# First feed-forward of a macaron layer in seven half products per gate/up tile, with its modulation vectors computed later

## Chip, cores and metric

One core of one Trainium2 chip runs the whole layer as one program. The metric is the time of one execution in microseconds (us), taken as the median of several; a profiled execution gives the rows shown below. TensorE (PE) multiplies, VectorE (DVE) and ScalarE (ACT) do the elementwise work, GpSimd (POOL) does some of it and issues a few DMAs, and SyncE (SP) issues most DMAs, in the order of its own queue.

## What is computed

The input is one sequence of 512 tokens with 1024 features in float32. Cut to what matters here:

```python
sc = silu(c)
mod = sc @ ada_w + ada_b                      # nine vectors of 1024: sh1 sc1 g1 sh2 sc2 g2 sh3 sc3 g3
y = rmsnorm(h, ffn1_pre_g) * (1 + sc1) + sh1
y = (silu(y @ w_gate) * (y @ w_up)) @ w_down  # 1024 -> 2816 -> 1024
h = h + 0.5 * g1 * rmsnorm(y, ffn1_post_g)
...                                           # token mixing with sh2 sc2 g2
...                                           # a second feed-forward with sh3 sc3 g3
```

The two feed-forwards have the same shapes and other weights. Matrix products keep nearly float32 accuracy by splitting each operand in a rounded part and a rest (hi, lo) and adding three products: hi·hi, hi·lo, lo·hi.

## The kernel before

**Three multiplications for one.** `mm3` (L112) issues three matmuls, at L113, L114 and L115. `unit` (L97) loads 512 KB of weights on SP's queue into one of four `raw` buffers (pool `wraw`), casts them to `hi` on ACT (L108) and subtracts to `lo` on DVE (L109); `hi` and `lo` have four buffers each in the pool `wsp`.

**Order of work.** The kernel is written as one program; a scheduler places the instructions of each engine from that order and from when it thinks that data are ready, so instructions of a later step can stand ahead of those of an earlier one. On each engine they run strictly in the order placed. The `GAP_` constants pad pools and so shift addresses.

**Modulation vectors.** `ada(s, kind, j)` (L120) makes 128 entries of one vector: one DMA of 512 KB into a `raw` buffer, four multiply-and-sum instructions on DVE (L134) and one reduction (L138). There are 72 of them. `ada_scale` (L140), `gate_rows` (L146, writes the gate vector to DRAM) and `gate_load` (L154, reads it back for all partitions into the buffer `G`) finish a vector.

**First feed-forward** (`ffn1`, L313).
- Start: `prep(k)` (L324) makes feature block k of y from two `ada` calls, transposes on PE and two ACT instructions (L332, L334); the lo part follows on DVE (L335). Meanwhile the six gate/up blocks of the first three of 22 tiles of 128 hidden features (`START_F = 3`) are multiplied block by block (`first`, L339; results `ps_s`). Their weights park in `wsp` buffers and their split parts in the tail of `hT`.
- 19 further tiles (`up_tile`, L235): two weight blocks of 1024x128, 48 matmuls with 512 columns each (`pua`). `swiglu_evac` (L224) applies sigmoid and two multiplications and splits the result at once into `hT[0]` and `hT[1]`. After each tile one entry of the list `rest` runs, at some two: 24 entries in all, most of them an `ada`.
- `down` (L244): the output columns in two halves, each of 11 units of two hidden tiles by four token blocks (24 matmuls of 512 columns a unit). Each unit takes another entry of `rest`.

**Token mixing** (`mix`, L399): 24 projections `pft` of 24 matmuls each, between which chains of small steps for eight heads run on all engines (`level`, L612, with DVE L602 and L591 and POOL L603). Eight `ada` calls lie among them.

**Second feed-forward** (`ffn2`, L812): three tiles are made directly, with 256 columns at a time (`pub`). The other 19 use seven products of halves (`Tile`, L886): each of the seven is 4 blocks of 128 by `mm3` on 256 tokens, so 84 matmuls of 256 columns a tile. Needed for that are sums of quarters of y (`sums`, L833, into `Shi`, `Slo`; `sum4`, L858), sums of quarters of the weights (`prep1` to `prep5`, L913 to L936), and sums of the results (L946 to L974). The loop (L994) prepares tile v while it multiplies tile w:

```python
w.p6(); ...load...; v.prep1(); w.p5(); v.prep2(); w.p7(); v.prep3()
v.open(); v.p1(); v.p2(); v.prep4(); w.p4(); v.prep5(); w.p3()
```

The last two products (`p4`, `p3`) of the last tile are issued within `down`. There `hT` is one float32 tile, and `split` (L1025) makes hi and lo of two hidden tiles for each of the 22 units; the same two tiles are split again for the second half.

Of the kernel before, what the change touches and what calls it, by code (L numbers as in the profile page):

```python
# [7 lines left out]
F32 = mybir.dt.float32  # L8
F32R = mybir.dt.float32r
# [18 lines left out]
GAP_H = 128  # L28
# [6 lines left out]
def layer_kernel(ctx: ExitStack, tc: tile.TileContext, x, c, cols, gate_b,  # L35
# [48 lines left out]
    nc.scalar.activation(sg, crow, AF.Sigmoid)  # L84
    nc.vector.tensor_tensor(out=crow, in0=crow, in1=sg, op=ALU.mult)
    for q in range(2):
        pc = tr_tile(f"pc{q}")
        nc.tensor.matmul(pc, ident[0:2, q:q + 1].broadcast_to([2, P]), crow, start=True, stop=True)
        nc.vector.tensor_copy(sc[:, q * T:(q + 1) * T], pc)
# [134 lines left out]
    def swiglu_evac(f, psg, psu, hT, tag):  # L224
        t = small.tile([P, T], F32, tag="x2", name=f"t{tag}_{f}")
        nc.scalar.activation(t, psg, AF.Sigmoid)
        nc.vector.tensor_tensor(out=t, in0=t, in1=psg, op=ALU.mult)  # L227
        nc.vector.tensor_tensor(out=t, in0=t, in1=psu, op=ALU.mult)
        nc.scalar.copy(hT[0][:, f, :], t)
        nc.vector.tensor_tensor(out=hT[1][:, f, :], in0=t, in1=hT[0][:, f, :].bitcast(F32), op=ALU.subtract)  # L230

# [3 lines left out]
    def up_tile(f, wgu, y, hT, tag):  # L235
        us = [k3(unit(wgu[f, g], 1024, f"{tag}_{f}_{g}")) for g in range(2)]
        ps = [mm_tile(f"pu{tag}_{f}_{g}") for g in range(2)]
        for g in range(2):
            for k in range(KT):
                mm3(ps[g], (us[g][0][:, k, :], us[g][1][:, k, :]), (y[0][:, k, :], y[1][:, k, :]),  # L240
                    k == 0, k == KT - 1)
        swiglu_evac(f, ps[0], ps[1], hT, tag)

    def down(wd, hT, tag, s, nxt, n=NF, order=lambda f: f, pump=None, drain=None, rest=(), split=None):  # L244


        t0, ss0, later = [], [], []
        nu = n // 2
        for half in range(2):
# [12 lines left out]
            for u in range(nu):  # L262
                v = unit(wd[half, u], 1024, f"d{tag}_{half}_{u}")
# [3 lines left out]
                for _ in range(2 if split and u < 3 else 1):  # L267
                    if rest:
                        rest.pop(0)()
# [26 lines left out]
        return later  # L296
# [16 lines left out]
    def ffn1():  # L313
        with tc.tile_pool(name="hT1", bufs=1) as hp:
            phase(hp, "gap_h1", GAP_H)
            hT = (hp.tile([P, NF, T], F32R, name="hThi1"), hp.tile([P, NF, T], F32R, name="hTlo1"))
# [3 lines left out]
            for v in range(2 * START_F):  # L320
                sl = slice(NF - 2 * (v + 1), NF - 2 * v)
                dst.append(tuple(a[:, sl, :].rearrange("p a b -> p (a b)") for a in hT))

            def prep(k):  # L324
# [20 lines left out]
            def load(v, half):  # L345
                sl = slice(half * 512, (half + 1) * 512)
                unit(wgu1[v // 2, v % 2, :, sl], 512, f"s{v}_{half}", tuple(d[:, sl] for d in dst[v]),
                     park=("hi", "lo")[v % 2])

            nv = 2 * START_F  # L350
# [29 lines left out]
            for f in range(START_F):  # L380
                swiglu_evac(f, ps[2 * f], ps[2 * f + 1], hT, "a")
            rest = [lambda j=j: ada(0, 2, j) for j in range(KT)] + [lambda: gate_rows(0), lambda: ada(1, 0, 0), lambda: gate_load(0)]
            for s in (1, 2):
                rest += [lambda s=s, j=j, kind=kind: ada(s, kind, j) for kind in range(2) for j in range(KT)
                         if s + kind + j > 1]
                rest.append(lambda s=s: ada_scale(s))
# [5 lines left out]
            y2 = y_tiles(1)  # L392
            later = down(wd1, hT, "a", 0, (1, y2), rest=rest)
            while rest:
                rest.pop(0)()
        return y2, later


    def mix(y, later):  # L399
        with ExitStack() as mc:  # L400
# [388 lines left out]
            rest = [lambda j=j: ada(1, 2, j) for j in range(KT)] + [lambda: gate_rows(1), lambda: None, lambda: gate_load(1)]  # L789
            h_qf(0)  # L790
            for hd in range(NH):
                m_qk(hd)
                rest.pop(0)()
                h_g(hd)
                m_g(hd)
                rest.pop(0)()
                if hd + 1 < NH:
                    h_qf(hd + 1)
# [8 lines left out]
            y3 = y_tiles(2)  # L807
            later = down(w_out, (mhi, mlo), "m", 1, (2, y3), n=KT, order=order, pump=pump, drain=drain, rest=rest)
# [307 lines left out]
```

## Time and profile before

| what | value |
|---|---|
| median of three runs | 1036.87 us (1036.12 to 1037.81) |
| profiled execution, its own time | 1035.53 us |
| its span, first to last instruction | 1033.8 us |
| PE busy | 1011.2 us, 98% |
| DVE busy | 699.1 us, 68% |
| ACT busy | 431.0 us, 42% |
| granted TensorE clock, mean | 0.996 of full speed |

A busy share is an average over stages. A stage is bounded by the engine that has no idle time there; another engine's work costs nothing as long as it ends before the first one asks for it. An instruction's shown duration overlaps the next one's by some 0.07 to 0.1 us on DVE and ACT, and by much more on PE, so the distance between starts is what an instruction costs in a row of its kind.

### The profile page before, as it was taken

The numbers are of one execution on the slowest core, as the hardware profiler recorded it, in microseconds if no ns is written. First come the engines' busy times: TensorE is split into PE (matmuls) and PEld (weight loads), VectorE is DVE, ScalarE is ACT, GpSimd is POOL, SyncE is SP. The second block draws the span as 40 slices with busy tenths as digits, with TensorE's granted clock in tenths as the row PEclk, the third lists the DMA queues.
The fourth block names the chain that finished last, engine by engine and source line by source line (L and its number), as shares of the span: only waits on it lengthen the run. The fifth ranks groups of instructions, "written<-read, shape, count | busy, mean of one in ns | idle before, by whom it ended". The sixth has DMA issues, their size and how long they took to land.

```text
span 1033.8 us, 14910 instructions
## 1 busy us (share of the span) xinstructions
PE 1011.2 (98%) x5672; PEld 873.7 (85%) x5672; DVE 699.1 (68%) x1577; ACT 431.0 (42%) x694; POOL 86.6 (8%) x123
## 2 busy tenths in 40 slices
PE   6999999999999999999999999999999999999997
PEld 4788888888888887978888887889999999988886
DVE  7986455556655466279787786599687877983643
ACT  5532322332212155344434232466566666552531
POOL 1000000000000011012222222010010110000000
PEclk9999999999999999999999999999999999999999
DMA  9865444545554503253222421243445545563312
GB/s 344 281 220 159 143 163 135 171 151 173 188 200 147 170 34 116 90 174 133 80 85 101 104 82 42 62 144 94 114 130 143 133 125 140 159 200 122 102 42 81
DMA packets 45683, 141.49 MB, mean 137 GB/s; under 512 B 7974, under 2 KB 8358, under 8 KB 45612
## 3 DMA queue, kind: packets, MB, share of 16 engines
q1 hardware_dynamic: 42588, 135.41, 39.5%
q0 software_dynamic: 2736, 4.98, 3.1%
q8 instruction: 44, 0.72, 0.3%
q14 instruction: 27, 0.22, 0.1%
q10 hardware_dynamic: 288, 0.16, 0.1%
HBM read 138.41 MB, written 2.12 MB: 136 GB/s over the span
## 4 chain that ended last, share of the span: by engine, by line
PE 84%; DVE 9%; DMA 2%; issue 2%; ACT 1%; POOL 1%; DVEq 0%; POOLq 0%; SPq 0%; ACTq 0%
PE pua L114 7%; PE pua L113 7%; PE pua L115 7%; PE pft L114 4%; PE pft L113 4%; PE pft L115 4%; PE pdb L114 4%; PE pdb L113 4%; PE pdb L115 4%; PE pda L113 4%; PE pda L115 4%; PE pda L114 3%; PE pA L115 3%; PE pA L113 3%; PE pA L114 3%; PE pl L590 3%
## 5 line engine op out<-in xcount | busy, mean ns | idle before, releaser
L114 PE MATMUL pua<-ylo,h_a 128*128 128x512 f32 x304 | 119.8, 394 | 0.0
L113 PE MATMUL pua<-yhi,h_a 128*128 128x512 f32 x304 | 119.3, 392 | 0.0
L115 PE MATMUL pua<-yhi,l_a 128*128 128x512 f32 x304 | 118.0, 388 | 0.0
L108 ACT CAST h_a<-r_a 128x1024 fp32r<-128x1024 f32 x38 | 39.8, 1048 | 120.7 <-issue 76.9
L134 DVE CUSTOM_DVE_ANT_0 a<-a,sc 128x256 f32<-128x256 f32 x216 | 82.4, 423 | 0.0
L113 PE MATMUL pft<-yhi,h_ft 128*128 128x512 f32 x192 | 79.3, 413 | 0.0
L115 PE MATMUL pft<-yhi,l_ft 128*128 128x512 f32 x192 | 75.8, 395 | 0.0
L114 PE MATMUL pft<-ylo,h_ft 128*128 128x512 f32 x192 | 75.7, 394 | 0.0
L113 PE MATMUL pda<-h_da,hThi 128*128 128x512 f32 x176 | 69.5, 395 | 0.0
L115 PE MATMUL pda<-h_da,hTlo 128*128 128x512 f32 x176 | 69.0, 392 | 0.0
L113 PEld LDWEIGHTS pua<-yhi,h_a 128*128 128x128 f32 x304 | 57.1, 188 | 13.7 <-DVE ta L227 0.4
L114 PE MATMUL pda<-l_da,hThi 128*128 128x512 f32 x176 | 68.3, 388 | 0.0
L115 PEld LDWEIGHTS pua<-yhi,l_a 128*128 128x128 f32 x304 | 57.1, 188 | 12.8
L114 PEld LDWEIGHTS pua<-ylo,h_a 128*128 128x128 f32 x304 | 57.2, 188 | 11.3
L109 DVE TENSOR_TENSOR l_a<-r_a,h_a 128x1024 fp32r<-128x1024 f32 x38 | 46.4, 1222 | 24.1 <-ACT h_a L108 24.1
L108 ACT CAST h_da<-r_da 128x1024 fp32r<-128x1024 f32 x22 | 23.1, 1050 | 77.7 <-PE pda L115 58.5
L109 DVE TENSOR_TENSOR l_da<-r_da,h_da 128x1024 fp32r<-128x1024 f32 x22 | 26.9, 1224 | 33.2 <-ACT h_da L108 33.0
L911 DVE TENSOR_TENSOR l<-Ra,h 128x1024 fp32r<-128x1024 f32 x38 | 46.0, 1216 | 0.0
L910 ACT CAST h<-Ra 128x512 fp32r<-128x512 f32 x76 | 43.7, 618 | 3.6 <-PE pub L114 1.4
L134 DVE CUSTOM_DVE_ANT_0 a<-a,sc,col 128x256 f32<-128x256 f32 x48 | 23.2, 483 | 31.1 <-DMA a<-in_ada_w_dram 31.1
L113 PE MATMUL pA<-yhi,h 128*128 128x256 f32 x152 | 42.5, 280 | 0.9 <-ACT s L962 0.9
L115 PEld LDWEIGHTS pft<-yhi,l_ft 128*128 128x128 f32 x192 | 36.3, 189 | 8.3 <-DVE l_ft L109 0.2
(329 smaller groups left out, 2828.0 us busy)
## 6 DMA issues: line engine op xcount, KB each, us to landing
a<-in_ada_w_dram SPq DMA_DIRECT2D x70, 512.0 KB, 4.1
r_a<-in_wgu_dram SPq DMA_DIRECT2D x38, 512.0 KB, 4.2
r_ft<-in_w_ft_dram SPq DMA_DIRECT2D x24, 512.0 KB, 4.0
r_da<-in_wd_dram SPq DMA_DIRECT2D x22, 512.0 KB, 3.5
r_db<-in_wd_dram SPq DMA_DIRECT2D x22, 512.0 KB, 4.5
Rb<-in_wgu_dram SPq DMA_DIRECT2D x19, 512.0 KB, 3.5
Ra<-in_wgu_dram SPq DMA_DIRECT2D x19, 512.0 KB, 3.6
l<-in_wgu_dram POOLq DMA_DIRECT2D x19, 256.0 KB, 4.0
```

The costliest lines, as they stand in the source:

```text
L108: nc.scalar.copy(hi, raw)
L109: nc.vector.tensor_tensor(out=lo, in0=raw, in1=hi.bitcast(F32), op=ALU.subtract)
L113: nc.tensor.matmul(ps, lhs[0], rhs[0], start=start, stop=False, **kw)
L114: nc.tensor.matmul(ps, lhs[0], rhs[1], start=False, stop=False, **kw)
L115: nc.tensor.matmul(ps, lhs[1], rhs[0], start=False, stop=stop, **kw)
L134: nc.vector.tensor_tensor_reduce(out=raw[:, sl], in0=raw[:, sl], in1=sc[:, sl], scale=1.0, scalar=init if q == 0 else 0.0, op0=ALU.mult, o ...
L590: nc.tensor.matmul(pv[:, i, :], kk[:, sl], qq[:, sl], start=True, stop=True)
L910: nc.scalar.copy(hl[0][:, sl], raw[:, sl])
L911: tt(out=hl[1], in0=raw, in1=hl[0].bitcast(F32), op=ALU.subtract)
```

## The change

In the first feed-forward the 19 tiles go through the loop of seven products, which moves out of `ffn2` into a shared function `seven`. The sums of quarters of y are made from a float32 copy of y kept in the tail of `hT`. `hT` becomes one float32 tile, and both `down` phases split it through `splitter`, which keeps the parts of 7 of the 11 units for the second half. Of the modulation vectors, 12 `ada` calls and one `gate_rows` stay with the 19 tiles; the others move to `down` and to the mixing. The silu of c is one ACT instruction.

```diff
-    nc.scalar.activation(sg, crow, AF.Sigmoid)
-    nc.vector.tensor_tensor(out=crow, in0=crow, in1=sg, op=ALU.mult)
+    nc.scalar.activation(sg, crow, AF.Silu)
...
-    def swiglu_evac(f, psg, psu, hT, tag):
...
-    def up_tile(f, wgu, y, hT, tag):
...
+    def gated(f, ps, hT, tag):
+        t = small.tile([P, T], F32, tag="x2", name=f"sg{tag}_{f}")
+        nc.scalar.activation(t, ps[0], AF.Silu)
+        tt(out=hT[:, f, :], in0=t, in1=ps[1], op=ALU.mult)
...
+    def seven(hp, tag, f0, wgu, y, S, hT, sum4, ahead, extra):
...
+        W = [Tile(f) for f in range(f0, f0 + ahead)]
+        w, v = W[:2]
+        for fn in (w.load, v.load, w.prep1, w.prep2, sum4, w.prep3, w.prep4, w.prep5):
+            fn()
+        w.open()
+        w.p1()
+        w.p2()
+        for f in range(f0, NF - 1):
+            w, v = W.pop(0), W[0]
+            w.p6()
+            if f + ahead < NF:
+                W.append(Tile(f + ahead))
+            if f + 2 < NF:
+                W[1].load()
...
+            w.p3()
+            if extra:
+                extra.pop(0)()
...
+    def splitter(hp, tag, hT):
+        kept, room = {}, {}
+        def split(half, u):
+            if u in kept:
+                return kept[u]
...
+            if 3 <= u < 10:
+                kept[u] = hi, lo
+            src = hT[:, 2 * u:2 * u + 2, :]
+            nc.scalar.copy(hi, src)
+            tt(out=lo, in0=src, in1=hi.bitcast(F32), op=ALU.subtract)
...
     def ffn1():
-            hT = (hp.tile([P, NF, T], F32R, name="hThi1"), hp.tile([P, NF, T], F32R, name="hTlo1"))
+            raws = [s_tile(hp, t, f"raw{t}", dtype=F32).rearrange("p (v n) -> p v n", v=nv) for t in ("Shi", "Slo")]
+            hT = hp.tile([P, NF, T], F32, name="hT1")
...
+            for v in range(nv):
+                if v < 4:
+                    dst.append(tuple(wsp.tile(...)))
+                else:
+                    dst.append(tuple(hp.tile(..., tag=t, bufs=2) for t in ("X3h", "X3l")))
+            yf = hT[:, NF - KT:, :]
...
+            S = ffn_tiles(hp)
+            a11, a12, a21, a22 = (quarter(yf, th, kh) for th in range(2) for kh in range(2))
+            for n_, (p, q, op) in enumerate(((a21, a22, ALU.add), (r[:, 0], a11, ALU.subtract),
+                                             (a11, a21, ALU.subtract), (a12, r[:, 1], ALU.subtract))):
+                tt(out=r[:, n_], in0=p, in1=q, op=op)
+                if n_ < 3:
+                    nc.scalar.copy(S[0][:, n_], r[:, n_])
+                    tt(out=S[1][:, n_], in0=r[:, n_], in1=S[0][:, n_].bitcast(F32), op=ALU.subtract)
             for f in range(START_F):
-                swiglu_evac(f, ps[2 * f], ps[2 * f + 1], hT, "a")
+                gated(f, ps[2 * f:2 * f + 2], hT, "a")
...
-            for f in range(START_F, NF):
-                up_tile(f, wgu1, y, hT, "a")
-                rest.pop(0)()
-                if f % 4 == 0:
-                    rest.pop(0)()
-            later = down(wd1, hT, "a", 0, (1, y2), rest=rest)
+            extra = [lambda j=j: ada(0, 2, j) for j in range(KT)] + [lambda: gate_rows(0)] + mods[0][:4]
+            for n_ in (16, 13, 10, 7, 4, 1):
+                if n_ < len(extra):
+                    extra.insert(n_, lambda: None)
+            todo = seven(hp, "a", START_F, wgu1, y, S, hT, sum4, 2, extra)
+            rest = [lambda: None, lambda: gate_load(0)] + mods[0][4:] + mods[1]
+            y2, later = down(wd1, None, "a", 0, (1,), rest=rest, split=splitter(hp, "a", hT), pump=pump)
...
     def mix(y, later, mods):
             rest = [lambda j=j: ada(1, 2, j) for j in range(KT)] + [lambda: gate_rows(1), lambda: None, lambda: gate_load(1)]
+            rest = mods + rest
             for hd in range(NH):
                 m_qk(hd)
-                rest.pop(0)()
+                spend(2)
                 h_g(hd)
+                spend(1)
                 m_g(hd)
-                rest.pop(0)()
+                spend(2)
```

`mods[s]` is the list of 16 `ada` calls and one `ada_scale` of modulation s+1. `down` now takes one entry of `rest` per unit in both feed-forwards (`ffn2` took two in its first three units). The second feed-forward calls `seven` with `ahead=3` and an empty `extra`.

## Rows read from the trace of the kernel before

**Rows 1.** Busy time of each engine in five stretches of the span
```profile
core 0: us, PE busy (x) PEld busy (x) DVE busy (x) ACT busy (x) POOL busy (x), PEclk, DMA share, GB/s
27.00:55.10 28.10, 27.63 (x124) 21.65 (x124) 27.14 (x115) 16.20 (x24) 0.00 (x0) 1.00 0.81 280
55.10:263.80 208.70, 208.70 (x913) 171.24 (x913) 125.52 (x330) 60.99 (x79) 0.00 (x0) 1.00 0.50 163
436.10:622.00 185.90, 184.52 (x1023) 158.01 (x1022) 150.24 (x355) 72.30 (x102) 43.92 (x63) 0.99 0.34 108
717.30:902.60 185.30, 185.24 (x1575) 185.04 (x1574) 148.31 (x227) 116.97 (x237) 14.80 (x17) 1.00 0.49 136
902.60:960.00 57.40, 56.48 (x261) 46.71 (x260) 33.69 (x75) 22.01 (x26) 0.00 (x0) 1.00 0.48 154
```
**Rows 2.** Chain that ended last, by engine (part 4 of the page)
```profile
PE 84%; DVE 9%; DMA 2%; issue 2%; ACT 1%; POOL 1%; DVEq 0%; POOLq 0%; SPq 0%; ACTq 0%
```
**Rows 3.** Timeline of PE, 256-column matmuls: start us, us, engine, line, operation
```profile
712.74 0.28 PE L114 MATMUL pub<-ylo,h_b 128*128 128x256 f32 x1
...
717.27 0.28 PE L115 MATMUL pub<-yhi,l_b 128*128 128x256 f32 x1
...
730.28 0.28 PE L113 MATMUL pA<-Shi,h 128*128 128x256 f32 x1
...
735.81 0.28 PE L115 MATMUL pA<-yhi,l 128*128 128x256 f32 x1
```
**Rows 4.** Timeline of DVE over one tile of seven products
```profile
736.93 1.22 DVE L911 TENSOR_TENSOR l<-Ra,h 128x1024 fp32r<-128x1024 f32 x1
738.06 0.42 DVE L950 TENSOR_TENSOR g<-pB,s 128x256 f32<-128x256 f32 x1
740.37 0.42 DVE L972 TENSOR_TENSOR g<-pB,s 128x256 f32<-128x256 f32 x1 [1.89 <-PE pB L115]
740.90 0.69 DVE L973 TENSOR_TENSOR hT<-g 128x512 f32<-128x512 f32 x1
741.51 0.69 DVE L922 TENSOR_TENSOR Rb<-Rb 128x512 f32<-128x512 f32 x1
...
750.26 0.42 DVE L972 TENSOR_TENSOR g<-pB,s 128x256 f32<-128x256 f32 x1 [1.89 <-PE pB L115]
```
**Rows 5.** Timeline of DVE: one ada of the start, first and next instruction
```profile
33.16 0.48 DVE L134 CUSTOM_DVE_ANT_0 a<-a,sc,col 128x256 f32<-128x256 f32 x1
...
34.67 0.15 DVE L142 TENSOR_TENSOR modc<-modc,col 128x1 f32<-128x1 f32 x1
```
**Rows 6.** Timeline at the end of the start, DVE and ACT
```profile
47.72 1.23 DVE L109 TENSOR_TENSOR l_a<-r_a,h_a 128x1024 fp32r<-128x1024 f32 x1
...
49.46 0.77 ACT L332 ACTIVATE yhi<-pts,modc 128x512 fp32r<-128x512 f32 x1
50.13 0.77 ACT L334 ACTIVATE yfs<-pts,modc 128x512 f32<-128x512 f32 x1
```
**Rows 7.** Timeline of PE, last matmul of the first three tiles
```profile
54.77 0.40 PE L115 MATMUL ps_s<-yhi,hTlo 128*128 128x512 f32 x1
```
**Rows 8.** Waits from 55 to 264 us: total us, times, longest
```profile
DVE a L134 <- DMA a<-in_ada_w_dram: 46.9, 20, 8.4
```
**Rows 9.** Timeline of ACT and PE, start of the second down projection
```profile
903.80 1.05 ACT L108 CAST h_db<-r_db 128x1024 fp32r<-128x1024 f32 x1 [3.35 <-DMA r_db<-in_wd_dram]
...
905.17 0.39 PE L113 MATMUL pA<-yhi,h 128*128 128x256 f32 x1 [0.92 <-ACT s L962]
```
**Rows 10.** Token mixing: timeline of POOL and DVE, and PE's only wait
```profile
525.98 0.81 POOL L603 TENSOR_TENSOR kk<-kk,tb 128x256 f32<-128x256 f32 x1 [3.29 <-PE pl L590]
...
526.23 0.85 DVE L134 CUSTOM_DVE_ANT_0 a<-a,sc 128x256 f32<-128x256 f32 x1
527.00 0.08 DVE L134 DVE_READ_ACCUMULATOR2_ANT part<- 128x1 f32 x1
...
PE pvm L524 <- DVE rowb L517: 1.4, 1, 1.4
```

More of the change, by code (lines that the diff above doesn't have):

```diff
@@ L221, in y_token_tile @@
             hook(i, yfs)
-    def swiglu_evac(f, psg, psu, hT, tag):
[L225 to L230, printed above, removed]
     def k3(u):
         return tuple(v.rearrange("p (k n) -> p k n", k=KT) for v in u)
-    def up_tile(f, wgu, y, hT, tag):
[L236 to L242, printed above, removed]
+    HT = T // 2
@@ L262, in down @@
             for u in range(nu):
+                if nxt is not None and half == 1 and u == nu - 1:
+                    nxt = (nxt[0], y_tiles(nxt[0]))
+                    made.append(nxt[1])
                 v = unit(wd[half, u], 1024, f"d{tag}_{half}_{u}")
@@ L266, in down @@
                     v = (*v, split(half, u))
-                for _ in range(2 if split and u < 3 else 1):
-                    if rest:
-                        rest.pop(0)()
+                if rest:
+                    rest.pop(0)()
                 if u < nu - 4 or (drain and half == 0):
@@ L295, in down @@
                     later.append(lambda i=i, nn=nn, **kw: y_token_tile(nxt[0], i, nxt[1], nn, **kw))
-        return later
+        return (made[0], later) if made else None
     def post(tag, s, i, t0, ps, ss0, final):
@@ L346, in load @@
                 sl = slice(half * 512, (half + 1) * 512)
-                unit(wgu1[v // 2, v % 2, :, sl], 512, f"s{v}_{half}", tuple(d[:, sl] for d in dst[v]),
-                     park=("hi", "lo")[v % 2])
-            nv = 2 * START_F
+                raw = raws[half][:, v, :]
+                nc.sync.dma_start(raw, wgu1[v // 2, v % 2, :, sl])
+                nc.scalar.copy(dst[v][0][:, sl], raw)
+                tt(out=dst[v][1][:, sl], in0=raw, in1=dst[v][0][:, sl].bitcast(F32), op=ALU.subtract)
             prep(0)
@@ L400, in mix @@
+        return y2, later, rest
+    def mix(y, later, mods):
         with ExitStack() as mc:
@@ L877, in ffn2 @@
                     if hf == 1:
-                        t = small.tile([P, T], F32, tag="x2", name=f"sg_{f}")
-                        nc.scalar.activation(t, ps[f][0], AF.Silu)
-                        tt(out=hT[:, f, :], in0=t, in1=ps[f][1], op=ALU.mult)
+                        gated(f, ps[f], hT, "b")
                 if hf == 0:
@@ L1013, in ffn2 @@
[L1013 to L1017 removed]
+            todo = seven(hp, "b", FF2_F, wgu2, y, (Shi, Slo), hT, sum4, 3, [])
             def pump():
@@ L1021, in pump @@
                     todo.pop(0)()
-            hd = [s_tile(t, 32).rearrange("p (c a b) -> p c a b", c=3, a=2) for t in ("Shi", "Slo")]
-            def split(half, u):
-                c = (half * (NF // 2) + u + 3) % 5
-                if c < 3:
-                    hi, lo = hd[0][:, c], hd[1][:, c]
-                else:
-                    hi, lo = (hp.tile([P, 1024], F32R, tag=t, name=f"hs{t}{half}_{u}", bufs=2)
-                              .rearrange("p (a b) -> p a b", a=2) for t in ("X3h", "X3l"))
-                src = hT[:, 2 * u:2 * u + 2, :]
-                nc.scalar.copy(hi, src)
-                tt(out=lo, in0=src, in1=hi.bitcast(F32), op=ALU.subtract)
-                return hi, lo
-            rest = [lambda j=j: ada(2, 2, j) for j in range(KT)] + [lambda: gate_rows(2), lambda: None, lambda: gate_load(2)]
-            down(wd2, None, "b", 2, None, rest=rest, split=split, pump=pump)
+            rest = [lambda j=j: ada(2, 2, j) for j in range(KT)] + [lambda: gate_rows(2), lambda: gate_load(2)]
+            rest = rest[:1] + [lambda: None] + rest[1:]
+            down(wd2, None, "b", 2, None, rest=rest, split=splitter(hp, "b", hT), pump=pump)
     ffn2(*mix(*ffn1()))
```

286 lines of the change are left out of this document (144 added, 142 removed).

## Prediction, made before the result was known

> **What bounds the kernel now.** I read the busy time by stretches first. From 55.1 to 263.8 us, the 19 gate/up tiles of the first feed-forward, PE has no idle time at all, and DVE is busy for 125.5 of 208.7 us [rows 1]. The 19 tiles of the second feed-forward, already in seven products, stand from 717.3 to 902.6 us: 185.3 us, PE again full, DVE busy for 148.3 us [rows 1]. The chain that ended last agrees: PE holds 84% of it [rows 2]. So PE time removed from this stage shortens the run, as long as DVE, which gets more work, stays below PE. To judge that I read the timelines of PE and DVE in the second feed-forward, which show what the new loop costs tile by tile, and the end of the start stage, where the new loop has to begin.
>
> **The 19 tiles.** Before, a tile is 48 matmuls of 512 columns: 208.7 / 912 = 0.2288 us each, 10.98 us a tile [rows 1]. After, it is 7 x 4 x 3 = 84 of 256 columns. Two distances between starts of such matmuls are in the trace: 4.53 us / 40 = 0.1133 us in the three tiles made directly, and 5.53 us / 47 = 0.1177 us in the loop of seven products [rows 3]. The loop's own tile takes 750.26 - 740.37 = 9.89 us [rows 4], which is 84 x 0.1177. I take this value, since it is the same code with the same tiles; 0.1133 is kept for a rival. The loop as a whole then needs the 185.3 us of its twin [rows 1] instead of 208.7 us, minus 23.4 us. The last tile's `p4` and `p3`, 24 matmuls of 0.1177 us, lie in `down` in both kinds of loop and come back there: plus 2.8 us. **Net -20.6 us.**
>
> The trace disagrees with a rule here. A full-width 256-column matmul costs 0.1177 us against half of 0.2288, so halving the columns costs 3% in rate. The Trainium skill (TensorE: Matmul & The Clock Gate, section Back-to-back issue gap) gives columns / 2.4 GHz plus 2.5 ns, 109.2 and 215.8 ns, by which the same term would be an estimated 19 x (48 x 0.2158 - 84 x 0.1092) = 22.5 us.
>
> **The entry into the loop.** Before, PE's last matmul of the first three tiles starts at 54.77 us [rows 7] and the next tile follows at once, its weights split beforehand (DVE does such an l_a at 47.72 us [rows 6]). After, DVE first has to make S1 to S4 from the whole of y: four sums and three rests of 1024 elements. Such an operation costs 738.06 - 736.93 = 1.13 us [rows 4]; 7 x 1.13 = 7.9 us. They need block 7 of y, whose second ACT instruction ends at 50.13 + 0.77 = 50.9 us [rows 6]; without the casts for the next tiles ACT can start it after DVE's last ada work, before 47.72, plus two ACT instructions of 0.77 or less: 49.2 us. Taking 50.0 us, and in program order: the last lo part and three `gated` (four operations of 741.51 - 740.90 = 0.61 us [rows 4]: 2.4 us), the sums (7.9 us), `prep1` of the first tile (1.13 us) give 61.4 us for its first product, where PE is free at 55.0 us: a wait of 6.4 us. The scheduler places by readiness and can put the sums that only p5 and p7 need later, but before p6 DVE still needs two sums and a rest, three `gated`, the four weight sums and two rests, 3.4 + 2.4 + 2.4 + 2.3 = 10.5 us, until 60.5 us, against a p6 due at 55.0 + 24 x 0.1177 = 57.8 us: at least 2 us. Upper end 8 us (sum4 also in front, 1.13 us). **I take +5 us**, nearer to the program order. The start itself gains nothing: DVE is busy for 27.1 of its last 28.1 us [rows 1] with the same `ada` calls and splits. The removed multiplication for silu(c) stands beside loads at the very beginning: 0.
>
> **Does DVE keep up in the loop?** In the twin, DVE has one idle gap a tile, 1.89 us in which it waits for PE's last product [rows 4]. New are 12 `ada` calls in 18 tiles (a None stands in `extra` every fourth place), each 34.67 - 33.16 = 1.51 us of DVE [rows 5]. So DVE goes from 8.0 to 9.5 us of 9.89 in three tiles of four and stays below PE. Its weight rests for p6 are done at 738.06 us, and PE comes to the next p6 some 2 us later (730.28 + 9.89 = 740.17 us [rows 3]), so a delay of 1.5 us is covered; without this lead each one would cost its full length. Each of these `ada` also brings one 512 KB DMA onto SP's queue behind the loads `Ra` and `Rb`. Those load two and one tile ahead, and the raw buffers of the pool rotate past them, so I see no load late. `gate_rows` adds two tiny operations and a 4 KB write. **+1 us** (0 to 4).
>
> **The down projections.** For 15 of 22 units DVE and ACT now split hT: 1.13 us more on DVE, and about the same on ACT. A unit on PE is 24 x 0.2288 = 5.5 us; DVE's share is 1.13 + 1.13 + 1.51 = 3.8 us: hidden. In return `swiglu_evac` with its four DVE operations a tile is gone, hidden too. What does carry over is the twin's start of `down`: ACT waited 3.35 us for a weight load, and with it the copy that p4 needs, so PE stood 0.92 us [rows 9]. SP's queue before the first units is alike: **+0.9 us** (0 to 2). In the second feed-forward seven of 22 splits go, in PE's shadow, and gate 3 is loaded three units later, which only its own DVE operations after half 0 wait for: 0.
>
> **Token mixing.** Nine more `ada` calls, their 512 KB loads on SP's queue among the weights of `pft`, and one scale: 9 x 1.51 = 13.6 us of DVE, which has 185.9 - 150.2 = 35.7 us idle there [rows 1]. PE waits there only once, 1.4 us [rows 10], so the small chains have some slack, but an ada set ahead of a link can hold the heads' matmuls, and PE's whole queue behind them, by 1.5 us. Bounds 0 and 13.6; **+1.5 us**, near to 0 because eight such calls lie there now with no wait of PE named after them.
>
> An ada there can take longer: one of its four parts took 0.85 us at 526.23 us, while POOL ran from 525.98 us on [rows 10]; the first part of a normal one takes 0.48 us [rows 5]. The Trainium skill (SBUF — State Buffer, section Who interferes with whom) says that a DVE instruction with two inputs in SBUF contends with a GpSimd instruction that reads SBUF, and the second to issue blocks; this trace agrees with it. By that rule each of the nine could lose an estimated 0.4 us more, 3.6 us of DVE in all, still within the idle time.
>
> **Sum:** -20.6 + 5 + 1 + 0.9 + 1.5 = -12.2 us. Against the profiled execution's 1035.5 us that is 1023.3 us; the median of the runs is 1.3 us higher, 1036.9 us, so I forecast **1024.7 us**.
>
> **Rivals.**
> - Faster pitch. The loop in the first feed-forward keeps 0.1133 us per matmul: 84 x 0.1133 = 9.52 us a tile, 19 x 0.37 = 7 us less, **1017.7 us**. For it: the second feed-forward ran its first products at this pitch, and left it only later. Against: all full tiles of the loop there hold 9.89 us. 0.14.
> - DVE becomes the bound in the loop, and it gets slower. Place: an `ada` in DVE's strict order whose load has not landed holds the weight rests behind it. In the old loop DVE waited for such loads 20 times, 46.9 us, 2.3 us each [rows 8], at no cost, since it had idle time to spare. If that goes on, a tile with an ada needs 2.3 + 1.51 - 1.89 = 1.9 us more than PE: 12 x 1.9 = 23 us in place of the 1 us above, **1046.7 us**. It decides from an average wait of 0.38 us per ada on, and eats the whole forecast at about 1.4 us. Against: the loads can be issued most of a tile ahead. 0.08.
> - The mixing takes the nine `ada` on its path: 13.6 instead of 1.5 us, **1036.8 us**, no change. For: DVE at 81% there goes to 88%. Against: the one wait of PE. 0.06.
> - Several costs at their upper ends (entry 8, loop 4, down 2, mixing 4 us): **about 1034 us**. 0.10.
> - The forecast itself: 0.62.
>
> **Numbers.** About 0.2% (2 us) is what a measurement of this kernel can tell from no change. Faster by more: the forecast, the faster pitch, the upper ends and a little of the mixing case, 0.87; the same: most of the mixing case, 0.05; slower: DVE as the bound, 0.08. The range takes in the faster pitch with a cheap entry (1017.7 - 3) at the low end and the upper ends of the costs at the other: **1014 to 1035 us**.
>
> **What would show it.** Right: no `pua`, twice as many `pA` and `pB` matmuls, a tile every 9.9 us in the first feed-forward; a gap of PE of some 5 us before the first p1 and p6, ended by DVE; DVE there over 90% busy, its gap before L972's twin almost gone. Wrong: PE gaps that return in each tile with an ada, ended by DVE or a DMA; a tile nearer to 9.5 us; PE waits between `pl` matmuls in the mixing that now name DVE.

## The result, and the profile after

The median after is 1044.02 us (4 runs, 1041.7 to 1045.28) against 1036.49 us before on the same chip: ratio 1.007, 95% interval 1.0045 to 1.0095. The change makes the kernel **7.5 us slower**; 12.2 us faster had been forecast. The profiled execution took 1042.81 us, its span is 1041.0 us. Line numbers of the new kernel: L132 is the multiplication of `ada`, L150 the DMA of `gate_rows`, L283 and L284 the weight casts and rests, L295 to L298 the weight sums, L327 and L335 the copies of partial sums on ACT, L111 to L113 the matmuls.

Busy time of each engine in four stretches of the new kernel: the first feed-forward's loop (from its first p1 to the first `pda` matmul), its down projection, the token mixing, and the second feed-forward's loop:

```profile
core 0: us, PE busy (x) PEld busy (x) DVE busy (x) ACT busy (x) POOL busy (x), PEclk, DMA share, GB/s
56.50:262.50 206.00, 192.74 (x1573) 190.44 (x1572) 175.40 (x332) 120.34 (x249) 14.91 (x17) 0.97 0.61 155
262.50:389.10 126.60, 126.57 (x570) 103.53 (x569) 85.30 (x234) 47.57 (x67) 4.14 (x6) 1.00 0.50 160
439.20:630.40 191.20, 185.17 (x1034) 157.68 (x1033) 163.63 (x438) 75.92 (x104) 45.73 (x64) 1.00 0.44 130
724.80:909.90 185.10, 185.10 (x1574) 185.10 (x1573) 147.86 (x220) 118.07 (x237) 14.78 (x17) 1.00 0.53 136
```

The two loops run the same 1573 or 1574 recorded matmuls, the second in 185.1 us without a gap, the first in 206.0 us with PE idle for 13.3 us and a mean granted clock of 0.97. The old loop took 208.7 us [rows 1]. So the 23.6 us between 208.7 and 185.1 us did go from the matmuls, and 20.9 us of them came back inside the loop. The chain that ended last shows what came in:

```profile
PE 67%; DVE 18%; DMA 8%; issue 3%; ACT 2%; POOL 1%; SPq 0%; DVEq 0%; POOLq 0%; ACTq 0%
```

Before, PE had 84%, DVE 9%, DMA 2% [rows 2]. The waits of the loop, 55 to 264 us (us in total, times, longest):

```profile
DVE a L132 <- DMA a<-in_ada_w_dram: 20.9, 11, 9.9
ACT h_a L283 <- DVE RbRb L296: 11.2, 4, 8.0
PE pAa L111 <- ACT s3a L335: 6.0, 1, 6.0
PE pAa L111 <- ACT s12a L327: 2.2, 4, 1.5
PE pBa L111 <- ACT h_a L283: 2.1, 1, 2.1
PE pAa L111 <- ACT h_a L283: 2.0, 1, 2.0
```

The last two lines are the entry, at 59 and 61 us. The longest wait of the line above them, 1.5 us at 183 us, and the 6.0 us up to 193.6 us are a stall in mid-loop that no part of the prediction had at that place. Its chain can be read in the timelines of SP, DVE, ACT and PE (start us, us, engine, line; in brackets the idle time before and what ended it):

```profile
169.80 0.39 SPq L150 DMA_DIRECT2D gd<-modc  x1
177.37 0.33 SPq L124 DMA_DIRECT2D a<-in_ada_w_dram  x1
190.51 0.48 DVE L132 CUSTOM_DVE_ANT_0 a<-a,sc,bs 128x256 f32<-128x256 f32 x1 [9.86 <-DMA a<-in_ada_w_dram]
190.92 0.69 DVE L296 TENSOR_TENSOR RbRb<-RbRb,Raa 128x512 f32<-128x512 f32 x1
191.65 0.62 ACT L283 CAST h_a<-RbRb 128x512 fp32r<-128x512 f32 x1 [8.02 <-DVE RbRb L296]
193.21 0.36 ACT L335 COPY s3a<-pAa 128x256 f32<-128x256 f32 x1
193.62 0.58 PE L111 MATMUL pAa<-yhi,h_a 128*128 128x256 f32 x1 [5.96 <-ACT s3a L335]
```

SP sends the gate vector to DRAM at 169.80 us; an `ada` load issued at 177.37 us lands 13.1 us later. DVE stands 9.86 us in front of it, the weight sum L296 behind it is late, the cast that needs this sum holds ACT for 8.02 us, and behind the cast in ACT's order stands the copy that PE's p4 must wait for, a copy of results that were complete with p7's last matmul at 184.56 us. (Two of the expectations below place the stall before the p1 at 187 us; p1 and p2 run until then, and PE stands behind them.) The DMA issues of 169 to 185 us (KB each, median us from issue to landing) show that every load behind that write whose landing the trace has was late, where 3.4 to 6.1 us are usual in this kernel's two loops:

```profile
l_a<-in_wgu_dram POOLq DMA_DIRECT2D x2, 256.0 KB, 12.5
RbG<-in_wgu_dram SPq DMA_DIRECT2D x1, 512.0 KB, 14.8
a<-in_ada_w_dram SPq DMA_DIRECT2D x1, 512.0 KB, 13.1
gd<-modc SPq DMA_DIRECT2D x1, 4.0 KB
```

Both large stalls come with a stretch at half clock (PEclk 0.50, 1.2 instead of 2.4 GHz), 6.8 us long, in which PE does half the work. What is lost is half of PE's busy time there: 3.2 us in the first; 2.1 us in the second, which begins while PE still stands:

```profile
61.40:68.20 6.80, 6.38 (x26) 5.77 (x26) 5.48 (x8) 2.56 (x6) 0.00 (x0) 0.50 0.18 42
191.10:197.90 6.80, 4.28 (x20) 4.28 (x21) 6.80 (x14) 3.97 (x9) 0.00 (x0) 0.50 0.26 77
```

The token mixing is the other loss, 191.2 against 187.1 us. PE's one wait there [rows 10] is now five (439 to 631 us: us in total, times, longest):

```profile
PE pqk L906 <- DVE qk L869: 2.7, 1, 2.7
PE po L837 <- DVE Sh L751: 1.2, 1, 1.2
PE pmt L732 <- ACT h_ft L106: 1.0, 1, 1.0
PE pvm L717 <- DVE rowb L710: 0.8, 1, 0.8
PE pl L783 <- DVE qq L795: 0.3, 1, 0.3
```

### The profile page after: what moved, and what is told of

It reads as the page before. It is cut to its first block, busy times and chain, and to the rows that moved or that the text cites. A ratio compares the mean times of both kernels' runs of the same rounds, so it can differ in the third digit from the quotient of the medians.

```text
span 1041.0 us, 16618 instructions
## 1 busy us (share of the span) xinstructions
PE 999.7 (96%) x6356; PEld 894.7 (86%) x6356; DVE 776.3 (75%) x1700; ACT 499.9 (48%) x876; POOL 104.3 (10%) x142
## 4 chain that ended last, share of the span: by engine, by line
PE 67%; DVE 18%; DMA 8%; issue 3%; ACT 2%; POOL 1%; SPq 0%; DVEq 0%; POOLq 0%; ACTq 0%
DMA a<-in_ada_w_dram 6%; PE pdb L112 4%; PE pdb L111 4%; DVE a L132 4%; PE pdb L113 4%; DVE l_a L284 4%; PE pda L112 4%; PE pda L111 4%; PE pda L113 4%; PE pAb L112 3%; PE pAb L111 3%; PE pAb L113 3%; PE pft L111 3%; PE pft L112 3%; PE pft L113 3%
## 5 line engine op out<-in xcount | busy, mean ns | idle before, releaser
L132 DVE CUSTOM_DVE_ANT_0 a<-a,sc 128x256 f32<-128x256 f32 x216 | 83.0, 422 | 0.0
L111 PE MATMUL pft<-yhi,h_ft 128*128 128x512 f32 x192 | 79.1, 412 | 0.0
L113 PE MATMUL pft<-yhi,l_ft 128*128 128x512 f32 x192 | 75.7, 394 | 0.0
L111 PE MATMUL pAa<-yhi,h_a 128*128 128x256 f32 x152 | 43.8, 289 | 8.0 <-ACT s3a L335 6.0
L283 ACT CAST h_a<-Raa 128x512 fp32r<-128x512 f32 x76 | 44.2, 618 | 6.6 <-DVE Raa L298 6.0
L111 PE MATMUL pBa<-yhi,h_a 128*128 128x256 f32 x152 | 43.8, 288 | 2.7 <-ACT h_a L283 2.1
L284 DVE TENSOR_TENSOR l_b<-Rab,h_b 128x1024 fp32r<-128x1024 f32 x38 | 46.0, 1216 | 0.1
L283 ACT CAST h_b<-Rab 128x512 fp32r<-128x512 f32 x76 | 43.7, 618 | 3.4 <-PE pub L112 1.7
L111 PE MATMUL pAa<-Shi,h_a 128*128 128x256 f32 x152 | 43.2, 284 | 2.2 <-ACT s12a L327 2.2
L284 DVE TENSOR_TENSOR l_a<-Raa,h_a 128x1024 fp32r<-128x1024 f32 x38 | 45.2, 1216 | 0.0
L113 PE MATMUL pAa<-yhi,l_a 128*128 128x256 f32 x152 | 43.8, 288 | 0.2 <-DVE l_a L284 0.2
L112 PE MATMUL pAa<-ylo,h_a 128*128 128x256 f32 x152 | 43.5, 286 | 0.0
L113 PE MATMUL pBa<-yhi,l_a 128*128 128x256 f32 x152 | 43.3, 285 | 0.0
L112 PE MATMUL pBa<-ylo,h_a 128*128 128x256 f32 x152 | 43.3, 285 | 0.0
L113 PEld LDWEIGHTS pft<-yhi,l_ft 128*128 128x128 f32 x192 | 36.0, 188 | 8.3 <-DVE l_ft L107 0.2
L132 DVE CUSTOM_DVE_ANT_0 a<-a,sc,col 128x256 f32<-128x256 f32 x48 | 23.5, 490 | 25.7 <-DMA a<-in_ada_w_dram 25.7
```

Source lines behind the costliest of these rows:

```text
L111: nc.tensor.matmul(ps, lhs[0], rhs[0], start=start, stop=False, **kw)
L112: nc.tensor.matmul(ps, lhs[0], rhs[1], start=False, stop=False, **kw)
L113: nc.tensor.matmul(ps, lhs[1], rhs[0], start=False, stop=stop, **kw)
L132: nc.vector.tensor_tensor_reduce(out=raw[:, sl], in0=raw[:, sl], in1=sc[:, sl], scale=1.0, scalar=init if q == 0 else 0.0, op0=ALU.mult, o ...
L283: nc.scalar.copy(hl[0][:, sl], raw[:, sl])
L284: tt(out=hl[1], in0=raw, in1=hl[0].bitcast(F32), op=ALU.subtract)
```

## The experiments

The theory after the result: (1) the write of the gate vector, 1024 elements of 4 bytes, holds up the loads behind it, and an `ada` in DVE's order brings that to PE; (2) the entry costs its gaps and a stretch at half clock; (3) the `ada` calls moved into the mixing stand in its chains. The main rival was that `ada` loads are late in this loop in any case. In the table, **loop** is the time from the first p1 of the first feed-forward (in the kernel before, the first `pua`) to the first `pda` matmul; **gaps** the sum of what starts of successive matmuls in it lie further apart than usual, where that is over 0.3 us; **half clock** the length of its stretches at 0.5; **mixing** runs from the first `pft` to the first `pdm` matmul, each in the profiled execution. The ratio is to the kernel before in the same session (median there 1035.6 to 1036.5 us), with its 95% interval.

| kernel | median us | ratio | loop | gaps | half clock | mixing |
|---|---|---|---|---|---|---|
| before | 1036.49 | 1 | 208.9 | 0.0 | 0 | 187.1 |
| after | 1044.02 | 1.007 [1.0045, 1.0095] | 206.0 | 15.1 | 13.6 | 191.2 |
| write listed in the down projection | 1041.35 | 1.0055 [1.0035, 1.0076] | 203.5 | 12.9 | 10.2 | 194.6 |
| write as 8 rows | 1033.59 | 0.9983 [0.997, 0.9996] | 197.0 | 8.9 | 6.8 | 190.8 |
| no `ada` in the loop | 1031.46 | 0.996 [0.9937, 0.9983] | 193.3 | 5.2 | 6.8 | 194.2 |
| no moved `ada` in the mixing | 1034.64 | 0.9984 [0.9965, 1.0004] | 205.1 | 12.8 | 17.0 | 185.6 |
| write forced later | 1041.51 | 1.0049 [1.0031, 1.0066] | 205.2 | 14.8 | 13.7 | 193.0 |
| write and one `ada` | 1030.9 | 0.995 [0.9936, 0.9964] | 193.8 | 5.7 | 6.8 | 193.0 |
| entry reordered | 1038.89 | 1.0037 [1.002, 1.0054] | 201.3 | 11.1 | 10.2 | 192.8 |
| rows, and `ada` in `down` | 1028.79 | 0.9934 [0.9909, 0.9958] | 198.6 | 9.9 | 6.8 | 185.6 |
| before, write as 8 rows | 1035.92 | 1.0001 [0.9993, 1.001] | 208.9 | 0.0 | 0 | 186.7 |
| all three repairs | **1023.83** | 0.9882 [0.9868, 0.9895] | 193.1 | 5.3 | 3.4 | 185.6 |
| the same, sums on GpSimd | 1028.32 | 0.9919 [0.9905, 0.9932] | 198.6 | 7.9 | 6.8 | 185.6 |

The mixing has stretches of 3.4 us at half clock of its own in some of these traces: one in the kernel before, in the one with the write forced later, with the write and one `ada`, and with the entry reordered; two with the write listed in the down projection and with no `ada` in the loop. The rows with 192.8 to 194.6 us are the five new kernels that have them; each stretch costs about 1.7 us there.

**1. The write listed in the down projection: a miss.**

```diff
-extra = [ada(0, 2, j) for j in 0..7] + [gate_rows(0)] + mods[0][:4]
+extra = [ada(0, 2, j) for j in 0..7] + mods[0][:5]
-rest = [None, gate_load(0)] + mods[0][4:] + mods[1]
+rest = [gate_rows(0), None] + mods[0][5:7] + [gate_load(0)] + mods[0][7:] + mods[1]
```

> The write of gate 0 to DRAM (1024 elements of 4 bytes) leaves the first feed-forward's loop for the second step of its down projection, where the second feed-forward has it; its slot in the loop gets a thirteenth modulation load instead. Theory (the write clogs the loads behind it: they take 13 to 16 us instead of about 4): the PE stall of 6.1 us before p1 at 187 us, that of 1.7 us at 181 us and the stretch at half clock behind them (about 3.4 us lost) go, the window 54 to 262 us shrinks by 8 to 11.5 us, and the time falls from 1042 to 1031 to 1035 us. Rival (modulation loads in VectorE's order are late in the loop anyway, the write only happens to lie near): no gain, with one more of them 1042 to 1045 us.

1041.35 us, a loop of 203.5 us: 0.7 us under the rival's range. But the edit did not do what it says. The scheduler places by readiness, and SP's timeline has the write in the loop again:

```profile
171.06 0.39 SPq L150 DMA_DIRECT2D gd<-modc  x1
```

With it the stall came back, 3.9 us at 188.5 us. The run decides nothing between the two theories; its use is the warning that a place in the list is not a place in time.

**2. The write as 8 rows of 512 bytes.** The 128 x 8 gate values are transposed by TensorE and copied out of PSUM, so that each DRAM row of 128 values is one piece.

```diff
-gates[s] = dram; dma(gates[s] as "p (o j)", g)            # 128 x 8, 4 bytes each
+pg = transpose(g); row = copy(pg)                         # 8 x 128, one slot later
+gates[s] = dram; dma(gates[s] as "(o j) p", row)
```

> The write stays in the loop, one slot later, but as 8 rows of 512 bytes: the gate's 128 x 8 columns are turned by TensorE into 8 x 128 and copied out of PSUM first. Theory (it is the 1024 pieces of 4 bytes that clog the queue): loads around it take about 4 us again, the stall goes as in the run with the write moved, 1031 to 1035 us. Rival (any write to DRAM at that place, or the late modulation load behind it, holds the loop): 1041 to 1044 us.

1033.59 us, and the loop 197.0 us: no stall is left in mid-loop (the largest gap behind the entry is 1.2 us), nor a stretch at half clock there. DMA issues of 198 to 206 us, around the write at 200.3 us:

```profile
l_a<-in_wgu_dram POOLq DMA_DIRECT2D x1, 256.0 KB, 4.1
gd<-row SPq DMA_DIRECT2D x1, 4.0 KB
```

The same 4 KB no longer delay their neighbour. The theory's number came out. The Trainium skill (DMA: Bandwidth & Descriptors, Rules for kernel authors) says that a strided last dimension becomes one descriptor per element and should be rearranged to be contiguous. The trace agrees: of the 1171 packets from 169.6 to 172 us in the new kernel 1056 are under 512 bytes, close to the write's 1024 elements.

**3. No `ada` in the loop.**

```diff
-extra = [ada(0, 2, j) for j in 0..7] + [gate_rows(0)] + mods[0][:4]
+extra = [None] * 8 + [gate_rows(0)] + [None] * 4          # vectors set to zero
```

> Left out: the twelve modulation vectors computed in the first loop (the gate of the first feed-forward and four scales of the mixing are zero); the write of 1024 elements of 4 bytes stays where it is. Theory A (the clogged queue reaches TensorE through the modulation load that stands in VectorE's order ahead of the weight sums): the stall before p1 near 187 us falls from 6.1 to under 2 us, 1030 to 1034 us. Theory B (it reaches TensorE through the weight loads themselves and the accumulating load, which are as late, 15 us): 4 us of the stall or more stay, 1036 to 1041 us.

1031.46 us, gaps only at the entry. But with nothing left to wait for, the write went out at 50.8 us, ahead of the loop, so this does not tell theory A from B. What it does show is the floor: without write and `ada`, the loop takes 193.3 us, of which 5.2 us of gaps and 6.8 us at half clock are the entry's.

**4. No moved `ada` in the mixing.**

```diff
-rest = mods + rest
+rest = [None] * len(mods) + rest                          # vectors set to zero
```

> Left out: the modulation vectors of the second feed-forward that the change moved into the mixing (nine loads with five VectorE operations each, and their scaling; those values are zero); their slots stay empty, so everything else keeps its place. Theory (VectorE's extra work in the mixing is what made it 4.0 us longer, from 187.2 to 191.2 us): the mixing falls back to 187 to 188.5 us, and the time to 1038 to 1040 us. Rival (the mixing is longer for another reason, such as its own remaining modulation steps standing at other heads): mixing stays at 190 us or more, time within 1.5 us of 1042.

The mixing went to 185.6 us, and the time to 1034.64 us. Busy time of the engines in this kernel's mixing:

```profile
437.90:623.50 185.60, 184.10 (x1035) 157.63 (x1034) 149.85 (x356) 73.78 (x103) 47.03 (x64) 1.00 0.37 108
```

DVE's busy time is 13.8 us less than after (163.63), PE's idle time 4.5 us less. The theory's mechanism holds, and both numbers fall below its ranges: the cost is larger than the 4.1 us seen against before, 191.2 - 185.6 = 5.6 us. The kernel before had lost 1.7 us in its mixing to a stretch of 3.4 us at half clock, which hid that much of the comparison. One such place in the new kernel's DVE timeline (start us, us):

```profile
475.65 0.47 DVE L132 CUSTOM_DVE_ANT_0 a<-a,sc,col 128x256 f32<-128x256 f32 x1
...
476.39 0.84 DVE L132 CUSTOM_DVE_ANT_0 a<-a,sc 128x256 f32<-128x256 f32 x1
...
477.51 0.41 DVE L795 TENSOR_TENSOR qq<-qq,tb 128x256 f32<-128x256 f32 x1
477.85 0.68 DVE L869 SCALAR_TENSOR_TENSOR qk<-qk,cv 128x512 f32<-128x512 f32 x1
```

The four parts of one `ada`, 1.86 us from 475.65 to 477.51 us, stand in front of the product L869, for which `pqk` waits 2.7 us. The third part took 0.84 us, twice the usual, beside a POOL product of 0.87 us that began at 476.08 us.

**5. The write forced later.** The eighth gate vector itself is computed in the down projection, so the write cannot go earlier.

```diff
-extra = [ada(0, 2, j) for j in 0..7] + [gate_rows(0)] + mods[0][:4]
+extra = [ada(0, 2, j) for j in 0..6] + mods[0][:5]
-rest = [None, gate_load(0)] + mods[0][4:] + mods[1]
+rest = [ada(0, 2, 7), gate_rows(0)] + mods[0][5:7] + [gate_load(0)] + mods[0][7:] + mods[1]
```

> The run with the write moved did not move it: the scheduler issued it at 171.1 us, in the loop, as soon as the eighth gate vector was there. Here that eighth vector is computed in the first step of the down projection, and one vector of the mixing takes its slot in the loop, so the write cannot start before the down projection; the loop keeps twelve modulation vectors. Theory (the write of 1024 elements of 4 bytes clogs the loads behind it): no load in the loop takes over 6 us, the loop from p1 to the down projection falls from 206.0 us to 194 to 197 us, the time from 1042 to 1031 to 1035 us; the down projection hides the write as the second one does. Rival (modulation loads standing in VectorE's order are late in that part of the loop without it): the loop stays at 203 us or more, 1040 us or more.

1041.51 us: the time is the rival's, the trace is not. The write was issued at 240.78 us, still beside the loop's last tiles, and the stall went with it. From 160 to 240 us, where the new kernel lost 8 us, PE was busy for 79.26 of 80 us with the twelve vectors in the loop; then (DMA issues of 239 to 256 us; timelines of ACT and PE; busy time of a stretch):

```profile
l_a<-in_wgu_dram POOLq DMA_DIRECT2D x1, 256.0 KB, 15.6
gd<-modc SPq DMA_DIRECT2D x1, 4.0 KB, 13.0
```

```profile
256.23 1.04 ACT L106 CAST h_da<-r_da 128x1024 fp32r<-128x1024 f32 x1 [8.89 <-DMA r_da<-in_wd_dram]
...
259.12 0.58 PE L111 MATMUL pAa<-Shi,h_a 128*128 128x256 f32 x1 [6.18 <-ACT s12a L327]
```

```profile
254.90:265.10 10.20, 5.98 (x22) 5.41 (x23) 7.27 (x23) 6.02 (x9) 0.00 (x0) 0.50 0.99 334
```

A weight load of the down projection, issued 0.4 us behind the write, took 14.9 us. ACT stood 8.89 us in front of its cast, ahead of the copy that PE needed, and half clock came with it. So the rival falls: the loads are late where the write is. My place for the write was no better than the first.

**6. The write, and one `ada` ahead of it.**

```diff
-extra = [ada(0, 2, j) for j in 0..7] + [gate_rows(0)] + mods[0][:4]
+extra = [None] * 7 + [ada(0, 2, 7), gate_rows(0)] + [None] * 4   # the other vectors zero
```

> Left out: eleven of the twelve modulation vectors of the first loop (seven of the gate, four scales of the mixing; those values are zero). The eighth gate vector keeps its slot, so that the write of 1024 elements of 4 bytes is issued in the loop as before; the run without any vector had let it go at 50.8 us. Theory A (the clogged queue reaches TensorE only through a modulation load in VectorE's order behind the write): stall after the write under 2 us, loop 192 to 195 us, time 1029 to 1032 us. Theory B (the weight loads and the accumulating load are late themselves): a stall of 4 us or more stays, loop 198 to 203 us, time 1035 to 1040 us.

1030.9 us and a loop of 193.8 us, both in theory A's ranges. The write went out at 166.9 us, and the loads behind it were as late as in the new kernel (DMA issues of 166 to 172.5 us), yet PE has no gap at all from 150 to 195 us (second fence, busy time of that stretch):

```profile
Raa<-in_wgu_dram SPq DMA_DIRECT2D x1, 512.0 KB, 14.6
RbG<-in_wgu_dram SPq DMA_DIRECT2D x1, 512.0 KB, 14.2
l_a<-in_wgu_dram POOLq DMA_DIRECT2D x1, 256.0 KB, 14.7
```

```profile
150.00:195.00 45.00, 45.00 (x384) 45.00 (x384) 38.23 (x62) 28.93 (x60) 3.52 (x4) 1.00 0.66 147
```

Theory A: the loop's own loads run far enough ahead to bear 15 us. What carries the delay to PE is an instruction that is not urgent and waits for a late load ahead of urgent ones in a strict order, the `ada` here, the cast of `down` in experiment 5.

**7. The entry reordered.** p1 and p2 of the first two tiles come ahead of the sums of y.

```diff
-w.prep1, w.prep2, sum4, w.prep3, w.prep4, w.prep5; w.open, w.p1, w.p2    # the sums of y in front of all
+w.prep1, w.open, w.p1, w.p2, v.prep1, v.open, v.p1, v.p2,
+sums of y (the one for p6 first), w.prep2, w.prep3, w.prep4, w.prep5, sum4
```

> Only the entry into the loop is changed: p1 and p2 of the first two tiles are written ahead of the four sums of y, which come after them (the sum for p6 first). Theory (the entry loses 5.5 us of gaps and 3.4 us at half clock because VectorE and ScalarE make sums and their rests before the first weights): gaps at the entry fall to 1 to 3 us and the stretch at half clock goes or halves, time from 1042 to 1035 to 1039 us. Rival (the same work must be done before p6 in any case): the gap moves to p6 and keeps its size, 1041 to 1043 us.

1038.89 us. Gaps at the entry fell from 5.4 to 4.5 us, less than the theory wanted, but in five pieces of 1.4 us or less, and the half clock there from 6.8 to 3.4 us. The rest of the gain in the loop (201.3 us) is a mid-loop stall of 6.7 instead of 7.8 us and the small gaps, which this schedule does not have. The interval of the ratio overlaps that of the new kernel, so alone this repair is likely but not settled; run 9 shows it better.

**8. Rows, and the leftover `ada` in the first down projection,** two a step in its second half.

```diff
-if rest: rest.pop(0)()
+for _ in range(2 if tag == "a" and half == 1 and u < 10 else 1):
+    if rest: rest.pop(0)()
```

> Two repairs together: the gate written as 8 rows of 512 bytes (as in the run of that name, 1033.6 us) and the ten modulation steps left for the mixing done in the second half of the first down projection, two a step. Theory: the mixing falls from 190.8 to 186 to 187.5 us at no cost in the down projection, where VectorE is busy 67% of the time: 1027 to 1031 us. Rival (the down projection has no room for a second load a step: TensorE waits there): the mixing gains 4 us, the down projection loses 2 or more, 1031 to 1035 us.

1028.79 us. The mixing takes 185.6 us, the down projection 127.7 against 126.6 us. Of PE's waits in the mixing two stay, 1.0 and 0.5 us.

**9. All three repairs,** the edits of 2, 7 and 8 together.

> The three repairs together: gate 0 written as 8 rows, the ten modulation steps of the mixing in the first down projection, and p1 and p2 of the first two tiles ahead of the sums of y. Theory (the three losses are separate and add): the run with the first two gave 1028.8 us; the entry gives 1 us of gaps and 1.7 us of half clock on top, 1025 to 1027 us. Rival (with the entry shorter, VectorE is late in the tiles behind it): 1028 to 1030 us.

**1023.83 us**, faster than both kernels and 12.1 us below the one before. That this is within 1 us of the 1024.7 us of the prediction does not bear the prediction out, since three things were changed to get there; the expectation, 1025 to 1027 us, was missed on the fast side. Busy time of its engines in the first loop, the first down projection and the mixing:

```profile
56.20:249.30 193.10, 188.92 (x1574) 187.12 (x1573) 175.06 (x333) 121.17 (x249) 14.95 (x17) 0.99 0.61 167
249.30:376.20 126.90, 126.66 (x571) 103.47 (x570) 98.64 (x316) 47.92 (x67) 4.16 (x6) 1.00 0.58 197
425.80:611.40 185.60, 184.11 (x1034) 157.61 (x1033) 149.78 (x356) 73.78 (x102) 46.98 (x64) 1.00 0.38 108
```

The entry has 4.1 us of gaps and 3.4 us at half clock. The step from run 8 is 5 us, more than the 2.7 us expected: the small gaps in the loop also fell, from 3.7 to 1.2 us; why is not shown.

**10. The same, two sums of y on GpSimd.**

```diff
-tt(out=r[:, 2], in0=a11, in1=a21, ...); tt(out=r[:, 3], in0=a12, in1=r[:, 1], ...)
+nc.gpsimd.tensor_tensor(out=r[:, 2], ...); nc.gpsimd.tensor_tensor(out=r[:, 3], ...)
```

> As the run with the three repairs, and two of the four sums of y at the entry (those for p7 and p3) are made by GpSimd, which is idle there, instead of VectorE. Theory (VectorE's queue bounds the entry): gaps at the entry fall by another 1 to 2.3 us and the stretch at half clock may go, 1022 to 1026 us. Rival (GpSimd's sums of 1024 elements take about 4 us each and come late for p7, or slow VectorE): no gain or up to 3 us slower than the run without.

1028.32 us, 4.5 us slower than run 9, more than the rival allowed. The two sums take GpSimd 2.91 and 2.38 us, not 4, and DVE instructions beside them took longer (timelines of POOL and DVE):

```profile
31.99 2.91 POOL L585 TENSOR_TENSOR hT<-hT 128x1024 f32<-128x1024 f32 x1 [20.18 <-ACT hT L527]
32.55 2.63 DVE L132 CUSTOM_DVE_ANT_0 a<-a,sc 128x256 f32<-128x256 f32 x1
...
58.36 2.38 POOL L588 TENSOR_TENSOR hT<-hT 128x1024 f32<-128x1024 f32 x1 [23.46 <-DVE hT L582]
...
59.53 3.42 DVE L298 TENSOR_TENSOR l_a<-Raa,h_a 128x1024 fp32r<-128x1024 f32 x2
```

The first sum was placed in the start, where DVE is busy for 28.3 of the 29.2 us from 27 us to the first p1 in run 9, and there one part of an `ada` took 2.63 instead of 0.42 us. The first p1 comes 1.3 us later (57.5 against 56.2 us), which fits this loss. The second sum ran beside two rests that PE waits for: 3.42 us for the pair instead of 2.35 us in run 9, and PE's wait grew from 0.83 to 1.92 us. A half clock of 6.8 instead of 3.4 us came with it; that these waits brought it is likely, not shown. The Trainium skill (SBUF — State Buffer, Who interferes with whom), which the prediction drew on for the mixing, agrees again: two SBUF inputs on DVE against GpSimd.

**11. The kernel before, with the write as rows.**

```diff
-gate_rows(0), ada(1, 0, 0), gate_load(0)                  # 4 bytes each
+gate_cols(0), [gate_put(0), ada(1, 0, 0)], gate_load(0)   # 8 rows of 512 bytes
```

> The kernel before with one edit: its gate 0 is written as 8 rows of 512 bytes instead of 1024 elements of 4 bytes. Theory (the old loop held its split weights units ahead, so late loads never reached TensorE there): the loads behind the write take 4 us instead of 9, but the time stays within 1.5 us of the kernel before. Rival (the write cost the old loop several us as well): 3 us or more faster than before.

1035.92 against 1035.91 us. In the kernel before the write did delay loads (DMA issues of 94 to 115 us in its trace), but PE had no gap in that loop:

```profile
r_a<-in_wgu_dram SPq DMA_DIRECT2D x3, 512.0 KB, 6.4
gd<-modc SPq DMA_DIRECT2D x1, 4.0 KB, 9.6
```

The write had been free there. The change made it cost, by putting it into a loop in which DVE has 5% of slack (busy for 175.4 us, against 185.1 us of PE's work) and strict orders lead straight to PE.

## Why the prediction was wrong

Against the forecast's 1023.3 us for the profiled execution, the new kernel needs 1042.8 us, 19.5 us more. By the steps of the prediction:

- **The 19 tiles: right.** The pitch is that of the twin: the loop of every kernel with a repair is 185.1 us plus gaps plus half the stretch at half clock, to within 1 us (all repairs: 185.1 + 5.3 + 1.7 = 192.1, measured 193.1), but for the sums on GpSimd, where 2.2 us are left over. The rival with the faster pitch did not occur.
- **The down projection, +2.8 and +0.9 us: the sum near, the second term wrong.** It went from 122.6 to 126.6 us, +4.0 against 3.7. p4 and p3 are there, but the wait of 0.9 us is not: PE waits for nothing in this stage. Some 0.6 us are `pda` matmuls that start every 0.2301 instead of 0.2289 us, for a reason that is not shown. That the sum comes out is luck. (`swiglu_evac` had three operations on DVE, not four; nothing was priced on them.)
- **The entry, +5 us: the gaps right, the sum too small.** Gaps were 5.4 us, at p1 already, ended by ACT's casts rather than by DVE. Not in the step: 3.2 us lost at half clock beside them, and a first p1 1.4 us later than the old loop's start. Some 5 us of the miss.
- **"I see no load late. `gate_rows` adds two tiny operations and a 4 KB write": this is the step that failed.** I priced the write by its bytes. Its 1024 pieces made the loads behind it 9 to 16 us long; at one of the twelve `ada` DVE stood 9.86 us, and PE lost 7.8 us and 2.1 us more at half clock. Small gaps elsewhere in the loop sum to 1.9 us, against +1 predicted for all of it. Some 11 us of the miss.
- **Token mixing, +1.5 us: right in kind, mis-sized.** 4.1 us against before, 5.6 us as the experiment isolates it. The prediction argued from eight `ada` calls there without a wait of PE; the nine more came at other places, one in front of a product that PE waits for. Some 3 us of the miss.
- **The rival that came nearest** is DVE as the bound, 1046.7 us, given 0.08. Its mechanism, an `ada` in DVE's strict order whose load has not landed, is what the trace shows, but not as 12 equal waits of 1.9 us: ten of the eleven waits, 11.0 us together, left PE no more than the small gaps of 1.9 us, and the one behind the write did the rest. It lacked the cause, so it got little chance, and that its time lies within 3 us of the measured one is luck.

Of the signs named for being right, the pitch and a gap of some 5 us at the entry came, the gap ended by ACT; DVE was busy for 85% of the loop, not over 90%. Of the signs of being wrong, one came, waits in the mixing that name DVE; gaps in each tile with an `ada` and a tile near 9.5 us did not.

What stays open: why the pieces slow the packets of the loads behind them for some 10 us, after they themselves are sent, and whether their number, their size or their stride does it, which the write as rows changed together; and why the schedules with repairs differ in their small gaps.

## What to carry to other kernels

When a loop gets tighter, price again every DMA that lay in it, by its pieces and not by its bytes: write a column vector to DRAM through a transpose, or where nothing behind it is ordered ahead of the bound engine. Work that is not urgent and waits for a load belongs where its engine's queue has slack in time, not only in busy share; look at what stands behind it in that strict order. And count for each long gap of TensorE not only the gap, but half of TensorE's busy time in the stretch at half clock that the rows show beside it.

## What the runs showed of the hardware

- A write of 1024 elements of 4 bytes to DRAM slowed the loads beside it. After the pieces had gone (169.6 to 172 us) the DMA engines were busy without moving much (busy time of 172 to 182 us in the new kernel, and its packets):

```profile
172.00:182.00 10.00, 9.61 (x82) 9.41 (x80) 7.37 (x11) 5.45 (x12) 0.88 (x1) 1.00 0.67 31
DMA packets 78, 0.31 MB, mean 31 GB/s; under 512 B 1, under 2 KB 1, under 8 KB 78
```

  A share of 0.67 for 31 GB/s, where the undisturbed loop has 0.53 for 136 GB/s. The loads' own packets took long: by these rows an estimated 0.67 x 16 x 10 / 78 = 1.4 us each, against 0.61 x 16 x 193.1 / 10152 = 0.19 us in the loop with all repairs (10152 packets). Weight and `ada` loads issued within 12 us behind the write took 6.4 to 15.7 us instead of 3.4 to 6.1, in every loop where it stood, the old one too; as 8 rows of 512 bytes it did nothing of the sort. The other two gate vectors are written in elements of 4 bytes in every kernel here, the repaired ones too: where the landing is in the trace, these writes took 9 to 13 us.
- Single stalls of PE of 3.8 to 6.2 us in mid-loop each came with 3.4 to 10.2 us at half clock, which began during the stall or, in one run, 1.3 us after it; the single gaps of 0.3 to 1.2 us there did not. Moving the stall moved the half clock with it (191 to 198 us, then 255 to 265 us). At the entry the runs do not settle which pauses bring it: with all repairs half clock came at 59.5 us, behind gaps of 0.6 and 1.0 us; with the entry alone reordered the same two gaps brought none, and it came at 67.9 us, behind gaps of 1.4 and 0.7 us.
- A GpSimd sum of 1024 elements in 2.4 us lengthened two DVE rests beside it from 2.35 to 3.42 us; another, of 2.9 us, lengthened one part of an `ada` from 0.42 to 2.63 us.
